# Encoder layer on one core: output projection by seven block products, residual held in DRAM and added to by accumulating transfers

## The chip, the core and the metric

The kernel runs on one core of a Trainium2 chip. The metric is the device time of one execution, in microseconds (us). The kernel before takes 936.28 us, the median of three runs (934.78 to 938.19).

## The reference

One encoder layer is applied to two sequences (`x_prompt`, `x_sample`) that share the weights. Each has 1024 positions and 1024 channels, in float32:

```
def _layer(x, p, ...):
    h = _rmsnorm(x, g_pre)
    z = einsum('bsd,de->bse', h, w_in)              # 1024 -> 3072
    a_val, a_gate, b_u, b_B, b_C, b_gate = split(z, 6, axis=-1)
    ya = _pool_mixer(a_val, w_pool, pool_scale) * silu(a_gate)
    yb = _short_conv(b_u, b_B, b_C, conv_w) * silu(b_gate)
    o = einsum('bse,ed->bsd', concatenate([ya, yb], axis=-1), w_out)   # 1024 -> 1024
    x = x + _rmsnorm(o, g_post)
    gate = sigmoid(einsum('bsd,de->bse', x, w_ple_gate))               # 1024 -> 1024
    e = einsum('bsk,kd->bsd', p, w_ple) * gate
    return x + _rmsnorm(e, g_ple)
```

## The kernel before

**Layout.** All tensors lie transposed: channels on the 128 partitions, positions along the free axis. A sequence `s` (0 the prompt, 1 the sample) has `KD`=8 channel tiles of 128 and `NCH`=2 chunks of `C`=512 positions. A float32 product is made of three: every operand is split into a high part (a cast on ACT, L145) and the rest (a subtraction on DVE, L146), and high by high, high by low and low by high are three matmuls of 128x128 by 128x512 (L284, L285, L286). An activation operand of two such parts is a "unit". An input for a unit that comes from DRAM goes through a tile `s` of 128x512, and there are `SBUFS`=6 of these. Everything else on positions lies in a pool of `TBUFS`=38 tiles `t` of 128x1024, which the units share. Weights come as tiles `wraw` of 128x1024 (three buffers) and are split in halves `whl` (eight buffers, `AHEAD`=5 halves split ahead).

**Stage A**, the input projection with both mixers: twelve pairs of channel tiles per sequence. The first pair of the prompt is done plainly. All others go through `pair_seven` (L455): seven block products of 12 matmuls, 84 per pair and both chunks, where plain products take 96. Its activation operands are sums and differences of blocks of h (`KINDS`: n11, n21, z, t1, t3, t4, n22, four units each, made once for a sequence); its weights (`pair_halves`, L195) are seven split halves and four sums on DVE. `emit` (L434) takes the results from PSUM, three of four with an add on DVE (L439, L441). The sample's operands are computed behind the prompt's stage A, stored in DRAM (`kept_...`) and loaded and split into units (`load_unit`) within the prompt's last pair: 28 units that take the place of the 28 of the prompt, each after the last product that reads the old one. The result y of stage A goes to DRAM (`yd`, 16 stores on POOL's queue).

**Stages B and C** then go sequence by sequence, with both chunks of B ahead of both of C. `stage_b` (L636) is the plain output projection: 8 channel tiles of 24 matmuls per chunk, on units of y that were loaded from `yd`; ACT scales the result by g_post out of PSUM (L654) and squares it. `norm_b` (L659) gets one over the root of the mean square (`rstd`, a product with ones, L301), loads x again from DRAM (16 tiles of 512 KB in all on SP's queue), multiplies and adds on DVE (L670, L671), and splits the new residual x1 into units. `stage_c` (L718) is the gate: 24 matmuls per piece (a channel tile of a chunk), a sigmoid on ACT (L738), the product with the p-projection, which the opening of the kernel had left in DRAM (`pled`, L739), and a square. `norm_c` (L772) scales (L786), adds x1 (L791) and stores y on SP's queue. The last `TAIL`=3 pieces of the last chunk are worked off in halves of 256 positions, in an order written out by hand.

**What sets the order.** The code is a program in order; `load` puts transfers on SP's queue and `bg_dma` on POOL's, both in program order (`pinned`). Work that no product waits for soon (`norm_b`, `norm_c`, loads of operands) is written as generators in a list `bg`; `tick` advances the first of them by a step after each product, and `drain` runs them to the end. `w_out` and `w_gate` are loaded once per chunk, 32 tiles each in all.

## Time and profile before

| | |
|---|---|
| median of 3 runs | 936.28 us (934.78 to 938.19) |
| profiled execution, its own time | 934.77 us |
| span of that execution | 932.6 us |
| TensorE (PE) busy | 894.6 us, 96% |
| VectorE (DVE) busy | 706.8 us, 76% |
| ScalarE (ACT) busy | 485.6 us, 52% |
| GpSimd (POOL) busy | 55.1 us, 6% |
| mean granted TensorE clock | 0.991 |

The profile is of one execution, 1.5 us under the median. Its span is the time from the first to the last recorded instruction. Stage A of the prompt ends near 310 us of it, stage A of the sample near 546, and the four chunk stages of each sequence fill the rest up to about 915, where the last piece's norm and stores begin. A group of instructions is named by its line, engine, operation and tiles (out<-in); idle time is put down to what ended it.

### The profile page before, as it was taken

To read this page: it belongs to the slowest core of one execution; us is meant where nothing else is said; L and a number is where in the kernel's file an instruction comes from. 1 tells how busy PE (TensorE), PEld (TensorE's weight loads), DVE (VectorE), ACT (ScalarE), POOL (GpSimd) and SP (SyncE) were. 2 spreads that over 40 slices of the span, in tenths; PEclk is the share of its full clock that TensorE was granted. 3 is DMA by queue.
4 is the path that set the end of the run, shared out by engine and by line. 5 is a ranking of instruction groups with operands and counts; after the bars stand their busy time and mean duration, and the time that the engine had idled before them with its cause. 6 is when DMAs were issued, how large, how long until landed. Compare 5 with 4: busy or idle time off the path is not lost.

```text
span 932.6 us, 11021 instructions
## 1 busy us (share of the span) xinstructions
PE 894.6 (96%) x3902; PEld 721.3 (77%) x3902; DVE 706.8 (76%) x1083; ACT 485.6 (52%) x829; POOL 55.1 (6%) x122
## 2 busy tenths in 40 slices
PE   6999999999999999999999989999999999999991
PEld 4787888888887788888888868878888787888881
DVE  5799999989588887665766764377878685969767
ACT  6967764333345643334333355465663745675643
POOL 0111112130000000000000000000000000000003
PEclk9999999999999999999999999999999999999996
DMA  9742545662316622122211174526146567262532
GB/s 329 293 181 76 195 147 173 217 238 84 112 48 202 226 91 69 68 82 76 68 68 69 68 257 150 181 87 229 69 181 225 203 185 289 91 225 69 188 129 90
DMA packets 48982, 140.49 MB, mean 151 GB/s; under 512 B 5664, under 2 KB 9248, under 8 KB 48928
## 3 DMA queue, kind: packets, MB, share of 16 engines
q1 hardware_dynamic: 39632, 107.23, 33.5%
q0 software_dynamic: 9152, 32.51, 9.5%
q8 instruction: 30, 0.49, 0.2%
q14 instruction: 24, 0.20, 0.1%
q10 hardware_dynamic: 144, 0.05, 0.0%
HBM read 107.27 MB, written 32.51 MB: 150 GB/s over the span
## 4 chain that ended last, share of the span: by engine, by line
PE 82%; DVE 8%; DMA 4%; ACT 3%; issue 2%; SPq 0%; DVEq 0%; ACTq 0%
PE z L286 27%; PE z L285 27%; PE z L284 27%; DVE t L791 1%; DVE t L786 1%; DVE u L146 1%; ACT u L145 1%; DMA s<-kept_t 1%; DMA s<-yd 1%; DMA s<-kept_n 1%; DVE t L833 1%; DMA t<-p_d 1%; DVE t L739 1%; DVE whl L146 1%; DMA t<-pled 0%
## 5 line engine op out<-in xcount | busy, mean ns | idle before, releaser
L284 PE MATMUL z<-u,whl 128*128 128x512 f32 (+1 forms) x1212 | 471.1, 390 | 4.8 <-ACT s L475 2.1
L285 PE MATMUL z<-u,whl 128*128 128x512 f32 (+1 forms) x1212 | 470.5, 389 | 1.4 <-DVE u L146 1.4
L286 PE MATMUL z<-u,whl 128*128 128x512 f32 (+1 forms) x1212 | 471.1, 389 | 0.5 <-DVE whl L146 0.5
L284 PEld LDWEIGHTS z<-u,whl 128*128 128x128 f32 x1212 | 227.2, 188 | 58.4 <-ACT s L475 3.4
L285 PEld LDWEIGHTS z<-u,whl 128*128 128x128 f32 x1212 | 227.6, 188 | 53.9 <-DVE u L146 2.8
L286 PEld LDWEIGHTS z<-u,whl 128*128 128x128 f32 x1212 | 227.7, 188 | 51.3 <-DVE whl L146 0.9
L146 DVE TENSOR_TENSOR whl<-wraw,whl 128x512 fp32r<-128x512 f32 x201 | 135.3, 687 | 46.3 <-ACT whl L145 45.7
L145 ACT CAST whl<-wraw 128x512 fp32r<-128x512 f32 x201 | 122.2, 620 | 73.7 <-PE z L286 63.7
L145 ACT CAST whl<-wsum 128x512 fp32r<-128x512 f32 x92 | 56.2, 620 | 70.8 <-PE z L286 35.7
L146 DVE TENSOR_TENSOR whl<-wsum,whl 128x512 fp32r<-128x512 f32 x92 | 62.8, 687 | 37.0 <-ACT whl L145 36.5
L145 ACT CAST u<-t 128x512 fp32r<-128x512 f32 (+1 forms) x105 | 61.6, 618 | 35.0 <-DVE t L671 12.8
L146 DVE TENSOR_TENSOR u<-t,u 128x512 fp32r<-128x512 f32 (+1 forms) x105 | 67.8, 680 | 15.3 <-ACT u L145 15.2
L330 DVE TENSOR_TENSOR t<-t 128x512 f32<-128x512 f32 (+1 forms) x59 | 39.1, 662 | 34.7 <-ACT t L329 34.1
L146 DVE TENSOR_TENSOR u<-s,u 128x512 fp32r<-128x512 f32 x60 | 39.3, 687 | 7.5 <-ACT u L145 7.2
L654 ACT ACTIVATE t<-z,par_sb 128x512 f32<-128x512 f32 x32 | 22.1, 689 | 44.0 <-PE z L286 44.0
L145 ACT CAST u<-s 128x512 fp32r<-128x512 f32 x60 | 35.8, 619 | 14.6 <-DMA s<-yd 7.4
L202 DVE TENSOR_TENSOR wsum<-wraw 128x512 f32<-128x512 f32 x46 | 31.6, 687 | 10.1 <-DMA wraw<-w_in_d 9.7
L284 PE MATMUL z<-u 128*128 128x512 f32 x64 | 26.0, 406 | 9.5 <-ACT u L145 9.5
L468 ACT COPY s<-z 128x512 f32<-128x512 f32 x23 | 13.5, 587 | 41.3 <-PE z L286 39.4
L475 ACT COPY s<-z 128x512 f32<-128x512 f32 x23 | 13.5, 586 | 41.2 <-PE z L286 41.2
L739 DVE TENSOR_TENSOR t<-t,s 128x512 f32<-128x512 f32 (+1 forms) x35 | 21.9, 641 | 15.8 <-ACT s L738 12.0
L738 ACT ACTIVATE s<-z 128x512 f32<-128x512 f32 (+1 forms) x35 | 19.6, 559 | 24.4 <-PE z L286 24.3
(85 smaller groups left out, 723.1 us busy)
## 6 DMA issues: line engine op xcount, KB each, us to landing
wraw<-w_in_d SPq DMA_DIRECT2D x48, 512.0 KB, 3.4
wraw<-w_out_d SPq DMA_DIRECT2D x32, 512.0 KB, 4.0
wraw<-w_gate_d SPq DMA_DIRECT2D x32, 512.0 KB, 3.4
pled<-t POOLq DMA_DIRECT2D x16, 512.0 KB, 3.8
t<-x_d POOLq DMA_DIRECT2D x16, 512.0 KB, 4.7
yd<-t POOLq DMA_DIRECT2D x16, 512.0 KB, 3.2
s<-yd SPq DMA_DIRECT2D x32, 256.0 KB, 4.9
t<-x_d SPq DMA_DIRECT2D x16, 512.0 KB, 7.7
```

Of the source, the lines that this page charges most:

```text
L145: nc.scalar.copy(out=hi, in_=src)
L146: nc.vector.tensor_tensor(out=lo, in0=src, in1=hi.bitcast(F32), op=ALU.subtract)
L202: nc.vector.tensor_tensor(out=t, in0=a, in1=b, op=ALU.add)
L284: nc.tensor.matmul(ps, wk[:, 0, kw, :], hi, start=a, stop=False, skip_group_check=on)
L285: nc.tensor.matmul(ps, wk[:, 0, kw, :], lo, start=False, stop=False, skip_group_check=on)
L286: nc.tensor.matmul(ps, wk[:, 1, kw, :], hi, start=False, stop=z, skip_group_check=on)
L330: nc.vector.tensor_tensor(out=acc, in0=acc, in1=tmp, op=ALU.add)
L468: nc.scalar.copy(out=u, in_=y)
L475: nc.scalar.copy(out=g, in_=y)
L654: nc.scalar.mul(og[d], z[i], col(G_POST + d))
L738: nc.scalar.activation(out=g, in_=z, func=AF.Sigmoid)
L739: nc.vector.tensor_tensor(out=e, in0=e, in1=g, op=ALU.mult)
```

## The change

The output projection (stage B) is computed by `pair_seven` too: four pairs of channel tiles per sequence, 84 matmuls each for both chunks. The stages now run as A of the prompt, A of the sample, B of the prompt, B of the sample, C of the prompt, C of the sample. What is new beside the product:

- `y_steps` loads the two halves of y of a group back on POOL's queue, makes four differences on DVE and stores them in DRAM (`ykept`); `load_y` loads and splits the 28 units of a sequence, within the last pair ahead of its stage B (A of the sample's last pair for the prompt, B of the prompt's last pair for the sample). The units n11, n21 and n22 are negated y.
- `Out` takes the results of stage B. The prompt's o is stored in DRAM (`od`) and loaded again; the sample's stays in SBUF.
- `residual` copies x to `x1d` in DRAM (POOL's queue). `norm_b` multiplies o by g_post and rstd (one DVE instruction of 128x1024 per channel tile, L718) and adds it to `x1d` by an accumulating transfer on POOL's queue (`bg_add`, 16 of 512 KB). The units of x1 are loaded from `x1d` and split: those of the prompt's first chunk within the last pair of B of the sample, the rest within stage C of the prompt.
- `norm_c` scales e and adds it to `x1d` by accumulating transfers too (24 of 256 KB), then copies `x1d` to y from DRAM to DRAM on POOL's queue (12 of 512 KB). Only the last chunk's tail loads x1 and adds on DVE as before.
- In stage C of the prompt a tile of `w_gate` serves both chunks, so 24 tiles of it are loaded instead of 32, and 16 of `w_out` instead of 32. A tile of `pled` is fetched one piece earlier than before.

```
+    def bg_add(out, in_):
+        pinned(nc.gpsimd.dma_start(out=out, in_=in_, accum_op=ALU.add))
...
+        for stage, n in (("A", NPAIR), ("B", KD // 2)):
+            for s in range(NSEQ):
+                for j in range(n):
+                    yield stage, s, j
...
+    raw_order.extend(w_gate[d] for i in range(NSEQ + 1) for d in range(KD))
...
+    def y_steps(s, j):
+
+        top, bottom = T()[:, :L], T()[:, :L]
+        bg_dma(top, yd[s][j])
+        bg_dma(bottom, yd[s][j + H])
...
+        for kind, out, p, q in (("t3", t, b, d), ("t1", b, b, a), ("z", d, d, b), ("t4", c, c, d)):
+            pinned(nc.vector.tensor_tensor(out=out, in0=p, in1=q, op=ALU.subtract))
+            bg_dma(ykept[s][kind][j], out)
...
+    class Out:
...
+        def put(self, d, c, ps, add, neg):
+            if d not in self.o:
+                self.o[d] = [T()[:, :L], NCH]
+            o = halves(self.o[d][0])[c]
+            emit(o, ps, add, neg)
+            a = halves(self.acc)[c]
+            add_square(a, o, small() if self.begun[c] else None, not self.begun[c])
...
+            if not self.left:
+                bg.append(norm_b(self.s, self.acc, self.kept))
...
+        for k, o in enumerate([kept[k] for k in range(KD)] if kept else ahead_of(load_o, KD, 2)):
+            yield
+            pinned(
+                nc.vector.scalar_tensor_tensor(
+                    out=o, in0=o, scalar=col(G_POST + k), in1=r, op0=ALU.mult, op1=ALU.mult
+                )
             )
...
+            bg_add(x1d[s][k // 2][:, :, k % 2, :], o.rearrange("p (c t) -> p c t", c=NCH))
...
+    def load_x1u(s, c, us, ks=range(KD)):
+        for k in ks:
+            us.append(load_unit(x1d[s][k // 2][:, c, k % 2, :]))
             yield
...
-        for d in range(KD - tail):
+        for i, (d, c) in enumerate(order):
+            while len(x1u[s][c]) < KD:
+                tick()
             pump(AHEAD)
-            piece(d, 0, C, next_w())
-            tick(2)
+            if d not in ws:
+                ws[d] = next_w()
+            piece(d, c, 0, C, ws[d])
...
+        def out(k):
+            bg_dma(y[s, c, :, k : k + 2, :], x1d[s][k // 2][:, c])
...
+                if x1 is None:
+                    bg_add(x1d[s][k // 2][:, c, k % 2, :], e)
...
+    def take_place(stage, s, n):
+
+        kind = KINDS[n]
+        if stage == "B" and s:
+            for i in range(2):
+                next(first_x1u, None)
+            return
+        for i in range(H):
+            if stage == "A" and s == 0:
+                h[1][kind][i] = load_unit(kept[kind][i])
+            else:
+                yk[1 - s if stage == "A" else 1][kind][i] = load_y(1 - s if stage == "A" else 1, kind, i)
...
+    bg.appendleft(load_x1u(0, 1, x1u[0][1]))
+    bg.extend(load_x1u(1, c, x1u[1][c]) for c in range(NCH))
+    first = [(0, 0), (1, 0), (0, 1), (1, 1)]
+    stage_c(0, first + [(d, c) for d in range(2, KD) for c in range(NCH)], 0)
+    stage_c(1, [(d, 0) for d in range(KD)] + [(d, 1) for d in range(KD - TAIL)], TAIL)
```

The first place is POOL's own order. Before, from the last stores of y at the end of stage A up to the tail's arithmetic (a number behind a name is only the tile's):

```order
L119 DMA yd_6_115<-t 128x1024
L491 MEMSET t 128x8
L492 MEMSET t 128x8
L119 DMA yd_3_112<-t 128x1024
L119 DMA yd_7_116<-t 128x1024
L779 ISA
L779 TENSOR_TENSOR t<-t 128x256
L780 TENSOR_TENSOR t<-t 128x256
```

After, the stretch of stage B of the sample, where o of the prompt is loaded (L121) and added to the residual (L124):

```order
L121 DMA t<-od_117 128x1024
L121 DMA t<-od_118 128x1024
L121 DMA t<-od_119 128x1024
L124 DMA x1d_0_125<-t 256x1x512
L121 DMA t<-od_120 128x1024
L124 DMA x1d_0_125<-t 256x1x512
L121 DMA t<-od_121 128x1024
L124 DMA x1d_1_126<-t 256x1x512
L121 DMA t<-od_122 128x1024
L124 DMA x1d_1_126<-t 256x1x512
```

POOL had nothing in stages B and C; now a chain of loads, accumulating transfers and, later, copies to y runs on its queue through both.

The second place is SP's queue where stage C of the prompt begins. Before:

```order
L114 DMA wraw<-w_out_d 128x1024 x8
L114 DMA t<-x_d 128x1024 x4
L114 DMA wraw<-w_out_d 128x1024 x2
L114 DMA wraw<-w_gate_d 128x1024 x6
L114 DMA t<-pled_0_0_85 128x1024
L114 DMA t<-x_d 128x1024 x4
```

After, with the loads of x1 (s<-x1d) among the weights:

```order
L116 DMA wraw<-w_out_d 128x1024 x4
L116 DMA wraw<-w_gate_d 128x1024 x3
L116 DMA s<-x1d_0_125 128x512 x2
L116 DMA s<-x1d_1_126 128x512 x2
L116 DMA wraw<-w_gate_d 128x1024
L116 DMA s<-x1d_2_127 128x512 x2
L116 DMA s<-x1d_3_128 128x512 x2
L116 DMA wraw<-w_gate_d 128x1024 x2
```

The loads of x are gone; in their place SP's queue holds loads that wait for accumulating transfers, with weights behind them.

The third place is SP's queue ahead of the tail. Before:

```order
L114 DMA wraw<-w_gate_d 128x1024 x2
L114 DMA y_d<-t 128x512 x2
L114 DMA t<-pled_1_1_98 128x1024
L114 DMA y_d<-t 128x512 x6
L114 DMA t<-pled_1_2_99 128x1024
L114 DMA t<-pled_1_3_100 128x1024
L114 DMA y_d<-t 128x256 x16
```

After:

```order
L116 DMA wraw<-w_gate_d 128x1024 x2
L116 DMA t<-pled_1_2_99 128x1024
L116 DMA t<-pled_1_3_100 128x1024
L116 DMA t<-x1d_0_129 128x1024
L116 DMA t<-x1d_1_130 128x1024
L116 DMA t<-x1d_2_131 128x1024
L116 DMA t<-x1d_3_132 128x1024
L116 DMA y_d<-t 128x256 x16
```

The stores of y have left this queue, and the two loads of pled stand ahead of everything that waits there.

## Rows read from the trace of the kernel before

**Rows 1.** The page: engines over the span, and PE's busy tenths in 40 slices.

```profile
PE 894.6 (96%) x3902; PEld 721.3 (77%) x3902; DVE 706.8 (76%) x1083; ACT 485.6 (52%) x829; POOL 55.1 (6%) x122
...
PE   6999999999999999999999989999999999999991
```

**Rows 2.** Windows by stage; columns are named in the first line.

```profile
core 0: us, PE busy (x) PEld busy (x) DVE busy (x) ACT busy (x) POOL busy (x), PEclk, DMA share, GB/s
100.00:150.00 50.00, 50.00 (x218) 40.49 (x217) 47.68 (x66) 33.39 (x50) 7.57 (x16) 1.00 0.46 154
...
296.00:330.00 34.00, 31.63 (x133) 24.49 (x133) 29.90 (x49) 23.25 (x41) 1.29 (x6) 1.00 0.69 231
536.00:556.00 20.00, 16.26 (x67) 11.95 (x66) 11.49 (x17) 9.47 (x16) 0.53 (x1) 1.00 0.78 248
560.00:893.00 333.00, 332.87 (x1433) 267.86 (x1432) 240.90 (x386) 195.76 (x330) 0.00 (x0) 1.00 0.49 170
893.00:915.00 22.00, 17.90 (x148) 17.26 (x146) 11.45 (x25) 10.51 (x22) 0.00 (x0) 1.00 0.21 72
```

**Rows 3.** PE's waits, 296 to 330: waiting line, releaser, us, times, longest.

```profile
PE z L284 <- ACT s L475: 1.4, 2, 1.0
PE z L284 <- ACT s L468: 0.6, 1, 0.6
PE z L284 <- DVE t L441: 0.4, 1, 0.4
```

**Rows 4.** ACT's waits, 285 to 330.

```profile
ACT u L145 <- DMA s<-kept_t: 4.0, 4, 1.3
```

**Rows 5.** PE's waits, 530 to 560.

```profile
PE z L284 <- ACT u L145: 1.6, 2, 1.3
PE z L285 <- DVE u L146: 1.4, 1, 1.4
```

**Rows 6.** The chain that ended last, at 549: start, us, what.

```profile
549.37 4.24 DMA s<-yd
```

**Rows 7.** Groups by line and shape: xcount | busy us, mean ns | idle before.

```profile
L146 DVE TENSOR_TENSOR whl<-wraw,whl 128x512 fp32r<-128x512 f32 x201 | 135.3, 687 | 46.3 <-ACT whl L145 45.7
...
L439 DVE SCALAR_TENSOR_TENSOR t<-z,s 128x512 f32<-128x512 f32 x30 | 20.6, 686 | 6.1 <-PE z L286 6.0
L671 DVE TENSOR_TENSOR t<-t 128x512 f32<-128x512 f32 x32 | 21.2, 685 | 0.0
L145 ACT CAST u<-s 128x512 fp32r<-128x512 f32 x60 | 35.8, 619 | 14.6 <-DMA s<-yd 7.4
```

**Rows 8.** DMA issues: queue, count, KB each, median us to landing.

```profile
t<-x_d POOLq DMA_DIRECT2D x16, 512.0 KB, 4.7
...
s<-yd SPq DMA_DIRECT2D x32, 256.0 KB, 4.9
t<-x_d SPq DMA_DIRECT2D x16, 512.0 KB, 7.7
...
s<-kept_n SPq DMA_DIRECT2D x12, 256.0 KB, 2.8
```

**Rows 9.** Timelines, DVE at 292 and POOL at 86: start, us, instruction.

```profile
292.05 2.49 DVE L146 TENSOR_TENSOR u<-s,u 128x512 fp32r<-128x512 f32 x4
...
86.18 1.45 POOL L119 DMA_DIRECT2D t<-x_d  x2 [3.26 <-DVE u L146]
```

**Rows 10.** Timeline of the tail: start, us, instruction, in brackets the idle time before.

```profile
885.41 9.10 SPq L114 DMA_DIRECT2D y_d<-t  x6
894.56 0.95 SPq L114 DMA_DIRECT2D t<-pled  x2
899.11 1.03 DVE L739 TENSOR_TENSOR t<-t,s 128x512 f32<-128x512 f32 x2 [2.55 <-DMA t<-pled]
905.08 0.39 PE L301 MATMUL psn<-u,ones 128*128 128x256 f32 x1 [0.84 <-ACT u L145]
```

More of the change, by code (lines that the diff above doesn't have):

```diff
@@ L298, in rstd_steps @@
         split(u[:, 0, :n], u[:, 1, :n], acc)
-        yield
+        for _ in range(wait):
+            yield
         ps = psn.tile([P, C], F32, name="psn")[:, :n]
@@ L343, in halves, with rstd_l, ahead_of @@
         return [t[:, c * C : (c + 1) * C] for c in range(NCH)]
-    def rstd_l(acc, tmp, out):
+    def rstd_l(acc, tmp, out, wait=1):
         for c in range(NCH):
-            yield from rstd_steps(halves(acc)[c], halves(tmp)[c], halves(out)[c])
-    def ahead_of(make, n):
-        cur = make(0)
+            yield from rstd_steps(halves(acc)[c], halves(tmp)[c], halves(out)[c], wait)
+    def ahead_of(make, n, depth=1):
+        got = deque(make(i) for i in range(depth))
         for i in range(n):
-            nxt = make(i + 1) if i + 1 < n else None
-            yield cur
-            cur = nxt
+            if i + depth < n:
+                got.append(make(i + depth))
+            yield got.popleft()
     def stats_steps(s, out):
@@ L659, in norm_b, with __init__, use, done @@
-    def norm_b(s, c, og, acc, tmp, x1, x1u):
-        for j in range(KD // 2):
-            t = T()
-            load(out=t[:, : 2 * C].rearrange("p (k t) -> p k t", k=2), in_=x[s, c, :, 2 * j : 2 * j + 2, :]
+                if self.s:
+                    bg.append(y_steps(self.s, self.g))
+    class Out:
+        def __init__(self, s):
+            self.s, self.acc, self.o = s, T()[:, :L], {}
+            self.left = 2 * KD
+            self.begun, self.kept = [False] * NCH, {}
+        def use(self, j):
+            return lambda m, c, ps, add=None, neg=False: self.put(2 * j + m, c, ps, add, neg)
+        def put(self, d, c, ps, add, neg):
[5 more added lines that the diff above has]
+            add_square(a, o, small() if self.begun[c] else None, not self.begun[c])
+            self.begun[c] = True
+            self.o[d][1] -= 1
+            if not self.o[d][1]:
+                self.done(d, self.o.pop(d)[0])
+            self.left -= 1
+            if not self.left:
+                bg.append(norm_b(self.s, self.acc, self.kept))
+        def done(self, d, o):
+            if self.s:
+                self.kept[d] = o
+            else:
+                bg_dma(od[d], o)
@@ new lines, in norm_b, with load_o @@
+    def norm_b(s, acc, kept):
+        r = T()[:, :L]
+        yield from rstd_l(acc, T()[:, :L], r, 3 if s else 1)
+        def load_o(k):
+            o = T()[:, :L]
+            bg_dma(o, od[k])
+            return o
+        for k, o in enumerate([kept[k] for k in range(KD)] if kept else ahead_of(load_o, KD, 2)):
+            yield
+            pinned(
+                nc.vector.scalar_tensor_tensor(
+                    out=o, in0=o, scalar=col(G_POST + k), in1=r, op0=ALU.mult, op1=ALU.mult
+                )
@@ L788, in norm_c @@
                 )
-            for k in ks:
-                e = es[k][:, cs]
-                nc.vector.tensor_tensor(out=e, in0=e, in1=x1[k][:, cs], op=ALU.add)
-                (load if n < C else store)(y[s, c, :, k, cs], e)
+                if x1 is None:
+                    bg_add(x1d[s][k // 2][:, c, k % 2, :], e)
+            if x1 is None:
+                if j:
+                    out(j - 2)
+            else:
+                for k in ks:
+                    e = es[k][:, cs]
+                    nc.vector.tensor_tensor(out=e, in0=e, in1=x1[k][:, cs], op=ALU.add)
+                    load(y[s, c, :, k, cs], e)
             yield
-    def blank():
-        return [[None] * KD for c in range(NCH)]
+        if x1 is None:
+            out(KD - 2)
     def run(steps):
@@ L920, in tile_hybrid_encoder, with residual @@
     load_pools()
+    def residual(s):
+        for j in range(KD // 2):
+            bg_dma(x1d[s][j], x[s, :, :, 2 * j : 2 * j + 2, :].rearrange("c p k t -> p c k t"))
+            yield
+            yield
+            yield
     r1 = T()[:, :L]
@@ L937, in after @@
                 product_done(LATER)
-            for i in range(H):
-                h[1][kind][i] = load_unit(kept[kind][i])
+            take_place(stage, s, n)
         else:
@@ L958, in tile_hybrid_encoder @@
             continue
-        steps = pair_seven(h[s], use)
+        steps = pair_seven((h if stage == "A" else yk)[s], use)
         next(steps)
@@ L963, in tile_hybrid_encoder @@
             if n:
[L964 removed]
+                after(*q, n + 1)
             else:
[L966 to L967 removed]
+                after(*q, 0), after(*q, 1)
+            if stage == "A" and i == 2 and n == 1:
                 grp.pool()
```

210 lines of the change are left out of this document (99 added, 111 removed).

## The prediction

> **What bounds the kernel now.** I read the page first: which engine is busy, and when. PE works 894.6 of 932.6 us, and its row of tenths shows no hole in the middle; the rest is the start and the last slice [rows 1]. So what counts is the number of matmuls and the places where PE stands. The windows by stage [rows 2] give both. In a full stretch, 100 to 150, 218 matmuls take 50.00 us, 0.2294 us each, at a granted clock of 1.00, which is the upper of the two levels (2.4 GHz). From 560 to 893, all of stages B and C but the ends, PE is idle for 0.13 us of 333: nothing there waits, and nothing of DVE, ACT or DMA in it costs time as it lies. PE stands at three places after the start: 2.4 us at the hand-over from the prompt's stage A to the sample's (296 to 330), 3.7 us from stage A to stage B (536 to 556), 4.1 us in the tail (893 to 915).
>
> The waits name the causes. At the hand-over PE waits for ACT copies out of PSUM [rows 3], and these stand behind casts of units that wait for their loads (4.0 us at one kind [rows 4]). Between A and B, PE waits for the units of y [rows 5], and the chain there goes through a load of y of 4.24 us [rows 6]. In the tail two loads of pled stand on SP's queue behind six stores of y that hold it for 9.10 us; DVE waits 2.55 us for them, and the norm's product 0.84 [rows 10].
>
> I take the profiled execution as the base: 934.77 us, 1.5 below the median of 936.28.
>
> **Matmuls.** Stage B goes from 2 sequences x 2 chunks x 8 tiles x 24 = 768 to 2 x 4 pairs x 84 = 672, so 96 fewer. At 0.2294 us [rows 2] this is −22.0 us. It holds in full if the stretches stay as dense as 560 to 893 is now.
>
> **Other engines in stage B.** In a pair DVE has 7 splits, 4 sums of weights, 3 emits and 4 squares, 18 instructions x 0.69 us [rows 7] = 12.4 us, against 84 x 0.2294 = 19.3 us of PE. In stage A, 47.7 of 50 us of DVE hid under a full PE [rows 2]. The differences of y (32 instructions x 0.69 = 22 us) lie in stage A of the sample and in B of the prompt, where that slack covers them; the 32 multiplications and the 32 additions of norm_b now (0.685 each, L671's row standing for both [rows 7]) become 16 of twice the length. Cost 0. Without that cover it would be the 22 us, spread over two stages; I see no such place.
>
> **The gap from A to B.** The prompt's stage B no longer begins with y that has just been stored: it comes two stages later. The 3.7 us [rows 2] go, and the sample's y is loaded 4 pairs later as well. −3.7. What comes late next is the hand-over.
>
> **Two new hand-overs.** In the last pair ahead of each stage B, 28 units are loaded, cast and subtracted while their predecessors are read, as at the hand-over that exists now, where 28 units cost 2.4 us. The load on DVE is about the same: two pairs at 19 and 28 units, 66 instructions, at 0.62 us back to back (four in 2.49 [rows 9]) = 41 us, against 38.5 us of PE for two pairs. So there is a little more work than cover. Two things are heavier. The units n11, n21 and n22 come from `yd`, whose loads took 4.9 us where kept_n's took 2.8 [rows 8]. And in stage B the six `s` tiles also hold the squares and the copies of PSUM. Lower bound 0 (the units' casts get to DVE and ACT earlier than the products need them), upper bound worked out as a rival below. I take 3.0 us for each, nearest to the 2.4 us measured for the same 28 units: +6.0.
>
> **The waits on accumulating transfers.** SP's queue meets loads of x1 from B of the sample's last pair on; each waits until both adds of its tile have landed, and behind them stand the weights of stage C. The trace shows no accumulating transfer. Bounds for one of 512 KB, from issue to landing: 4.7 us if it is no dearer than a load of x of the same shape on POOL's queue, 9.6 us if it reads first and writes then, a load of 4.9 and another of 4.7 [rows 8]. I take 6, nearer to the lower end, as reading and writing can overlap; the highest row of 512 KB on any queue is 7.7 [rows 8].
>
> The first point where it can hurt: between the last multiplication of the prompt's norm_b and the split of its unit stand 25 instructions on DVE, x 0.60 us at the fastest = 15.0 us. Off go the issue on POOL (0.72, half of the pair's 1.45 [rows 9]), the unit's load (4.9 [rows 8]) and its cast (0.62 [rows 7]): 8.8 us are left for the add. Beyond that each us is paid at stage C's start. At 6 us it costs 0, at the upper bound of 9.6, 0.8. The adds before the last have more room; the sample's eight lie under stage C of the prompt, 16 pieces x 24 x 0.2294 = 88 us. POOL's issues are 0.72 us each, and nothing else needs that queue until the tail. The Trainium skill, page "Collectives: The Full Stack", section "The bandwidth ceiling: the fold count and why AG ≠ RS ≠ AR", says that an add in the DMA engines needs two reads of source and so runs at about half a copy's rate. By it an add would be an estimated 2 x 4.7 = 9.4 us, 0.6 over the margin, and the sum 0.6 higher; no run here shows it yet.
>
> **Stage C of the prompt** begins with two pieces of chunk 0, and then needs all eight units of chunk 1 for the third. Three of the eight can go through free `s` tiles ahead; the other five are loaded and split once the pieces have begun. PE needs a new unit every three matmuls, 0.69 us, and ACT and DVE can make one every 0.62 [rows 9], so only the first of the five can be late: it is needed 3 x 0.69 = 2.1 us into the third piece, and before it four instructions of the second piece's eviction (about 0.65 each, two of them on ACT) and its own cast and split (0.62 + 0.69 [rows 7]) are done, 3.9 us. That is 1.8 us late if all of it runs one after the other, and not late if two overlap. Bounds 0 and 2, I take the middle: +1.0. Shared tiles of w_gate lower the load on SP, DVE and ACT here, which I price at 0, as none of them bounds this stage [rows 2].
>
> **Loads that leave SP.** The 16 loads of x (7.7 us each, beside weights [rows 8]) and most stores of y leave its queue. No PE idle depended on them between 560 and 893, so 0.
>
> **The tail.** The pled tiles are fetched a piece earlier, ahead of what blocked them; the waits of 2.55 on DVE and 0.84 on PE [rows 10] go. On PE only the second lay on the way to the norm: −0.9, rounded with the issue. The end, 20 us of DVE and POOL arithmetic, keeps its form. What is new: POOL's adds and copies of chunk 0 stand ahead of its arithmetic in the tail, and the x1 that it adds must have come from DRAM. For chunk 0's adds two transfers of 256 KB and their issues, 2 x (0.55 x 6) + 1.8 = 8.4 us, lie under 4 pieces, about 22 us of PE. Cost 0.
>
> **Sum.** −22.0 −3.7 +6.0 +0.0 +1.0 −0.9 = −19.6 us. On the profiled execution 915.2; on the median 936.28 − 19.6 = 916.7, the forecast.
>
> **Rivals.**
>
> *The hand-overs stall on the `s` tiles.* 28 loads go through six tiles, of which squares and copies take one and a half to two and a half, so 3.5 to 4.5 are free. Each load holds its tile for its landing, its cast and its subtraction, 4.9 + 0.62 + 0.69 = 6.2 us [rows 7, 8]. 28 x 6.2 / 3.5 = 50 us, where about 38 of PE lie beside it: 12 us late, against 28 x 6.2 / 4.5 = 39 us, in time. For it: PE already waits behind such loads [rows 3, 4], and ACT waited 14.6 us over the 60 unit casts [rows 7]. Against it: with the same six tiles the hand-over costs only 2.4 us now. With +9 in B (against 3) and +5 in A (against 3), the time is 916.7 + 8 = 924.7.
>
> *The hand-overs are free.* y is in DRAM long before, so the loads wait for nothing but a free tile, and the pairs of stage B have no mixers beside them on DVE. Against it: the kept tiles of h lie ready now too, and PE still loses 2.4 us [rows 2]. Then −6.0: 910.7.
>
> *Slower: the accumulating transfers are slow.* One mechanism at one place: the adds of the prompt delay the units of x1 at the start of C, and those of chunk 0 of the sample delay the tail, through POOL's queue. With an add of L us for 512 KB, the first costs L − 8.8, the second 2 x 0.55 L + 1.8 − 23 where that is positive. It eats the gain of 19.6 from L of about 25 on (16.2 + 6.3 = 22.5). At L = 30 it is 21.2 + 11.8 = 33 us: 949. For it: no transfer here that reads and writes DRAM and adds has been seen, and the queue was idle before. Against it: the slowest transfer of this size, in the fullest stretch, took 7.7 us [rows 8], a third of the threshold.
>
> *No gain.* The 96 matmuls go, but waits of the same size take their place; that is the same two places with 20 us of stalls between them, and the time is 936. No row adds up to it.
>
> **How the numbers follow.** Forecast .62; hand-overs stall .18; hand-overs free .12; slow transfers .05; no gain .03. A measurement of this kernel can tell about 0.3%, 2.8 us, from no change. Faster by more: .62 + .18 + .12 = .92; within: .03; slower by more: .05. The range runs from 908 (910.7, less 1.0 for stage C at its lower bound and 2.55 − 0.84 = 1.7 if the whole of DVE's wait in the tail was on the path) to 928 (stalling hand-overs, and the ends of the unknown costs: 0.8 of the add, 1 of stage C, 1.5 of hand-over), leaving out the .05, the .03 and the edges of the others.
>
> **What would show it.** PE's matmuls 96 fewer, and the windows of stage B at 19.3 us a pair. PE idle at three hand-overs: near 2.4, 3 and 3 us, and its waits there naming ACT copies and unit casts. Landing of the adds against 8.8 us; no wait of SP for them that reaches PE at the start of C; at the third piece of C about 1 us. In the tail no wait of L739 for pled, and POOL's arithmetic not late. Wrong would be: a PE idle of more than 10 us anywhere after the start, a matmul of stage B dearer than 0.23 us, or an add over 10 us.

## The result, and the profile of the changed kernel

The changed kernel takes 971.46 us, the median of four runs (970.26 to 973.77), against 937.1 for four runs of the kernel before beside it: a ratio of 1.0373, interval 1.0344 to 1.0403. It is slower by 34 us, where the forecast was 20 us faster. The profiled execution has a span of 972.0 us, 39.4 more than the 932.6 of before.

The page of the changed kernel, as in [rows 1]; below them its granted clock in tenths:

```profile
PE 884.8 (91%) x3806; PEld 710.3 (73%) x3806; DVE 724.6 (75%) x1099; ACT 489.5 (50%) x833; POOL 139.9 (14%) x246
...
PE   6999999999999999999999989989599999089990
...
PEclk9999999999999999999999989999889999589995
```

The 96 matmuls are gone (3902 records before, 3806 now), but PE's share fell from 96 to 91%, and its row of tenths, which had no hole in the middle, now has a 5 and, further on, a 0 and an 8 side by side. Where PE stands, the granted clock falls with it: to 8 and to 5 tenths in the same slices.

The windows of the stretches that [rows 2] showed and of the new holes. Columns are as there: us, busy us and (in brackets) instructions of PE, PEld, DVE, ACT, POOL, then the granted clock, DMA share and GB/s:

```profile
296.00:330.00 34.00, 32.49 (x139) 25.38 (x138) 29.93 (x48) 22.41 (x40) 2.83 (x7) 1.00 0.81 269
...
530.00:560.00 30.00, 28.48 (x122) 22.41 (x121) 27.52 (x44) 21.42 (x38) 0.54 (x1) 1.00 0.74 232
560.00:600.00 40.00, 36.04 (x143) 28.40 (x142) 28.26 (x45) 18.81 (x34) 5.93 (x11) 0.91 0.53 191
...
680.00:720.00 40.00, 29.46 (x101) 22.44 (x100) 24.80 (x35) 12.07 (x22) 8.77 (x10) 0.83 0.84 186
...
760.00:800.00 40.00, 40.00 (x174) 32.39 (x173) 27.52 (x36) 20.59 (x31) 3.23 (x3) 1.00 0.55 137
800.00:840.00 40.00, 24.41 (x106) 19.43 (x104) 6.18 (x10) 6.22 (x11) 5.42 (x5) 0.84 0.66 127
840.00:880.00 40.00, 25.24 (x102) 20.12 (x103) 29.64 (x47) 29.62 (x47) 6.34 (x8) 0.77 0.69 188
```

A full stretch of 40 us holds 174 matmuls, 0.230 us each, as before. Two places fall far below it. One is 680 to 720, stage B of the sample, with 101 matmuls: 73 fewer, or 17 us. The other is 800 to 880, where stage C passes from the prompt to the sample, with 208 of 348: 140 fewer, or 32 us. PE's idle time is only part of that. In the second place PE is busy for 49.65 us with 208 matmuls, 0.24 us each, and up to 0.43 right behind the hole, where the granted clock is 0.50 (856 to 858), the lower level. A smaller hole, 560 to 600, lies ahead of all the adds and is taken up further down.

What PE waited for, 300 to 972 (waiting line, releaser, us, times, longest):

```profile
PE psn L308 <- ACT u L150: 34.2, 2, 30.4
PE z L290 <- ACT s L502: 6.7, 2, 3.8
PE z L290 <- DVE t L475: 5.9, 4, 4.0
PE z L292 <- DVE whl L151: 5.3, 2, 4.0
```

One wait of 30.4 us, for the cast of a norm's input on ACT, is most of the loss. Three views follow it back: ACT (790 to 860) stands at casts of units of x1 that wait for their loads, SP (690 to 860) at these loads, which wait for accumulating transfers, and POOL (690 to 860) between these transfers, for nothing that the profile shows:

```profile
ACT u L150 <- DMA s<-x1d: 42.3, 9, 6.9
...
SPq L116 <- DMA x1d<-t: 63.6, 10, 8.2
...
POOL x1d L124 <- issue: 51.6, 8, 9.8
```

POOL's timeline shows what that is (start, us, instruction, in brackets the idle time before it and what ended it). First the prompt's adds (`x1d<-t`, 512 KB) with loads of o between them, then some of the sample's, then the 256-KB adds of `norm_c`:

```profile
673.17 1.12 POOL L124 DMA_DIRECT2D x1d<-t  x1 [7.56 <-DVE t L718]
673.78 1.09 POOL L121 DMA_DIRECT2D t<-od  x1
679.88 1.11 POOL L124 DMA_DIRECT2D x1d<-t  x1 [5.01 <-issue]
...
686.71 1.10 POOL L124 DMA_DIRECT2D x1d<-t  x1 [5.14 <-issue]
...
774.17 1.08 POOL L124 DMA_DIRECT2D x1d<-t  x1 [48.05 <-DVE t L718]
...
827.99 1.10 POOL L124 DMA_DIRECT2D x1d<-t  x1 [5.66 <-issue]
865.46 2.62 POOL L124 DMA_DIRECT2D x1d<-t  x3 [36.37 <-DVE t L867]
```

Most adds of 512 KB come 6.7 to 7.3 us apart, of which POOL is busy for 1.1; three of the fourteen gaps are longer, up to 10.9 us. The sample's eight go from 774.2 to 828.0, 54 us. Three adds of 256 KB go out within 2.62 us. The DMA issues, answering [rows 8] (KB each, median us to landing):

```profile
x1d<-t POOLq DMA_DIRECT2D x16, 512.0 KB, 6.5
s<-x1d SPq DMA_DIRECT2D x32, 256.0 KB, 4.4
...
x1d<-t POOLq DMA_DIRECT2D x24, 256.0 KB, 8.7
```

The chain of waits shows the end of it (start, us, what): the last add, a load of x1 behind it, and the norm's product that PE had waited for since 824.4.

```profile
827.99 6.45 DMA x1d<-t
...
836.34 6.89 DMA s<-x1d
...
854.76 0.79 PE psn L308
```

An add lands 6.5 us after its issue (the median; 6.4 to 10.5). The prediction took 6. So the latency was right, and what was wrong is that the next one is not issued until then: in the sample's chain each goes out 0.3 us after the one before it has landed. In stage B of the sample it costs by another way: the loads of o stand on POOL's queue behind the adds, and DVE, in its fixed order, waits for them (672 to 730):

```profile
DVE t L718 <- DMA t<-od: 15.7, 5, 3.9
```

### The profile page after: what moved, and what is told of

Same layout as the page of the kernel before. It is cut to its first block, busy times and chain, and to the rows that moved or that the text cites. A ratio compares the mean times of both kernels' runs of the same rounds, so it can differ in the third digit from the quotient of the medians.

```text
span 972.0 us, 11143 instructions
## 1 busy us (share of the span) xinstructions
PE 884.8 (91%) x3806; PEld 710.3 (73%) x3806; DVE 724.6 (75%) x1099; ACT 489.5 (50%) x833; POOL 139.9 (14%) x246
## 4 chain that ended last, share of the span: by engine, by line
PE 62%; issue 18%; DVE 7%; DMA 6%; ACT 4%; POOL 2%; SPq 0%; DVEq 0%; POOLq 0%; ACTq 0%
PE z L290 21%; PE z L291 21%; PE z L292 21%; POOL x1d L124 2%; DVE u L151 1%; DMA s<-kept_t 1%; ACT u L150 1%; DMA t<-yd 1%; DVE t L927 1%; DMA s<-x1d 1%; DMA s<-ykept_t 1%; DMA x1d<-t 1%; DMA t<-p_d 1%; DVE t L647 1%; DVE t L867 0%
## 5 line engine op out<-in xcount | busy, mean ns | idle before, releaser
L290 PE MATMUL z<-u,whl 128*128 128x512 f32 (+1 forms) x1180 | 463.7, 394 | 18.1 <-ACT s L502 6.7
L292 PE MATMUL z<-u,whl 128*128 128x512 f32 (+1 forms) x1180 | 461.6, 392 | 5.8 <-DVE whl L151 5.8
L291 PE MATMUL z<-u,whl 128*128 128x512 f32 (+1 forms) x1180 | 461.7, 392 | 0.2 <-DVE u L151 0.2
L150 ACT CAST whl<-wsum 128x512 fp32r<-128x512 f32 x124 | 75.5, 619 | 98.0 <-PE z L292 45.8
L150 ACT CAST whl<-wraw 128x512 fp32r<-128x512 f32 x145 | 88.4, 619 | 54.3 <-PE z L292 46.0
L151 DVE TENSOR_TENSOR whl<-wraw,whl 128x512 fp32r<-128x512 f32 x145 | 97.9, 686 | 15.4 <-ACT whl L150 15.3
L151 DVE TENSOR_TENSOR u<-s,u 128x512 fp32r<-128x512 f32 x92 | 61.3, 688 | 59.6 <-ACT u L150 59.2
L151 DVE TENSOR_TENSOR whl<-wsum,whl 128x512 fp32r<-128x512 f32 x124 | 84.3, 687 | 27.4 <-ACT whl L150 26.7
L150 ACT CAST u<-s 128x512 fp32r<-128x512 f32 x92 | 55.2, 618 | 66.9 <-DMA s<-x1d 51.5
L124 POOL DMA_DIRECT2D x1d<-t x40 | 38.3, 1026 | 209.6 <-issue 67.4
L151 DVE TENSOR_TENSOR u<-t,u 128x512 fp32r<-128x512 f32 (+1 forms) x73 | 46.8, 679 | 10.7 <-ACT u L150 10.4
L336 ACT ACTIVATE s<-t 128x512 f32<-128x512 f32 (+1 forms) x59 | 35.7, 609 | 30.3 <-DVE t L800 15.0
L121 POOL DMA_DIRECT2D yd<-t x16 | 8.7, 543 | 236.7 <-DVE t L610 137.6
```

Source lines behind the costliest of these rows:

```text
L124: pinned(nc.gpsimd.dma_start(out=out, in_=in_, accum_op=ALU.add))
L150: nc.scalar.copy(out=hi, in_=src)
L151: nc.vector.tensor_tensor(out=lo, in0=src, in1=hi.bitcast(F32), op=ALU.subtract)
L290: nc.tensor.matmul(ps, wk[:, 0, kw, :], hi, start=a, stop=False, skip_group_check=on)
L291: nc.tensor.matmul(ps, wk[:, 0, kw, :], lo, start=False, stop=False, skip_group_check=on)
L292: nc.tensor.matmul(ps, wk[:, 1, kw, :], hi, start=False, stop=z, skip_group_check=on)
```

## The experiments

The theory after these readings, Q: POOL's queue holds an accumulating transfer until the one before it has landed, and the chain of eight, mostly 6.8 us apart, is what PE waits for. The rival, M: memory and DMA engines are slow there for all transfers. Times are medians beside the kernel before on the same chip, which took 935.3 to 936.3 us in all five groups of runs. A time that stands without a ratio is one execution; repeated executions of one kernel lay 4 to 12 us apart here, so a few us between single ones prove nothing. Diffs are against the changed kernel unless another is named.

### Plain stores in place of the adds

```
-            bg_add(x1d[s][k // 2][:, :, k % 2, :], o.rearrange("p (c t) -> p c t", c=NCH))
+            bg_dma(x1d[s][k // 2][:, :, k % 2, :], o.rearrange("p (c t) -> p c t", c=NCH))
```

> The changed kernel with the 16 accumulating transfers of norm_b (512 KB each) made plain stores of the same shape to the same place; the residual is left out of x1, everything else is done. Theory Q: an accumulating transfer holds POOL's queue until the one before it has landed, so 16 of them go one after the other, 6.8 us apart, and that chain makes PE wait 30.4 us for the norm ahead of stage C of the sample and about 10 us in the last pairs of stage B of the sample. Then the stores are issued within about 1.5 us of each other, both stalls go, and the time falls from 971 to 920 to 930 us. Rival M: the memory and the 16 DMA engines are what is slow there (share 0.6 to 0.84 in these windows); then stores of the same bytes stay more than 4 us apart, and the time stays over 955.

It took 921.24 us. POOL's timeline, at the sample's stores:

```profile
759.83 0.68 POOL L121 DMA_DIRECT2D x1d<-t  x1 [3.79 <-DVE t L718]
761.03 0.68 POOL L121 DMA_DIRECT2D x1d<-t  x1 [0.52 <-DVE t L718]
762.45 0.67 POOL L121 DMA_DIRECT2D x1d<-t  x1 [0.75 <-ACT whl L150]
...
774.03 0.68 POOL L121 DMA_DIRECT2D x1d<-t  x1 [5.13 <-DMA t<-pled]
```

The first stores follow DVE at 1.2 to 1.4 us, and the stretch from 720 to 880 is full of matmuls. The last one was held too, until the fifth had landed at 773.7: three plain stores were on their way then (the load of pled that the line names is none of its inputs). So stores of these bytes are not slow there, as M had it; a store moves less than an add, though, and the run with rows of 4 KB below settles M with the adding left in. Without the adds' pace the kernel is where the forecast had put it, within 4.5 us.

### The sample's adds alone

```
-            bg_add(x1d[s][k // 2][:, :, k % 2, :], o.rearrange("p (c t) -> p c t", c=NCH))
+            (bg_dma if s else bg_add)(x1d[s][k // 2][:, :, k % 2, :], o.rearrange("p (c t) -> p c t", c=NCH))
```

> The same edit for the sample's eight transfers of norm_b alone (its residual is left out of x1); the prompt's eight still accumulate. By Q only the stall of 30.4 us ahead of the sample's stage C goes, with the low clock behind it: 935 to 942 us, and the stalls between 680 and 710 stay as they are. By M it stays over 960.

934.53 us, 0.5 under the range that Q gave. The prompt's adds still come some 6.8 us apart there. So of the 50.2 us between 971.5 and 921.2, these runs give 36.9 to the sample's eight adds and 13.3 to the prompt's eight. When the starts of the same matmuls are compared in the three traces, it is 32 and 13: some 5 us of the 36.9 were lost by 600, ahead of any add. Nearly all of that is the hole of 560 to 600, behind a load of y that landed 7.5 us after its issue and here 4.9.

### Adding in SBUF

```
+            xk = T()[:, :L]
+            bg_dma(xk.rearrange("p (c t) -> p c t", c=NCH), x[s, :, :, k, :].rearrange("c p t -> p c t"))
...
+            pinned(nc.vector.tensor_tensor(out=o, in0=o, in1=xk, op=ALU.add))
-            bg_add(x1d[s][k // 2][:, :, k % 2, :], o.rearrange("p (c t) -> p c t", c=NCH))
+            bg_dma(x1d[s][k // 2][:, :, k % 2, :], o.rearrange("p (c t) -> p c t", c=NCH))
```

> norm_b adds in SBUF again: x is loaded on POOL's queue beside o, DVE adds (16 instructions of 128x1024, 1.28 us each, 20 us in all), and x1 goes to DRAM by a plain store; the copy of x to DRAM ahead of it goes. Seven block products, the order of the stages and norm_c stay as changed. By Q both stalls go and DVE's 20 us are hidden: 918 to 932 us, faster than before (937) by 1 to 2%. By M the loads of x in the same place keep the stalls: over 950.

942.65 us, ratio 1.0105 (1.0047 to 1.0163). The adds' pace was gone, and yet the time stayed 21 us over that with plain stores; the expected range was missed. The windows of that run (columns as above) show that the loss in stage B of the sample stayed, while that at 800 to 840 is small:

```profile
680.00:720.00 40.00, 28.97 (x109) 22.18 (x110) 30.51 (x42) 14.97 (x27) 8.63 (x13) 0.83 0.80 266
...
800.00:840.00 40.00, 36.56 (x153) 29.25 (x152) 30.96 (x50) 27.74 (x46) 3.56 (x4) 0.96 0.74 221
```

DVE's additions wait in order for x (5.3 us at two of them) and PE once 8.5 us for a result that ACT takes out of PSUM late. The two loads and one store per tile on POOL's queue put a wait where the add had been. In the traces 15 us of the loss lie in stage B of the sample and 5 at the norm ahead of its stage C; why they are so large is settled no further than that.

### Adds of half the size

```
-            bg_add(x1d[s][k // 2][:, :, k % 2, :], o.rearrange("p (c t) -> p c t", c=NCH))
+            for c in range(NCH):
+                bg_add(x1d[s][k // 2][:, c, k % 2, :], halves(o)[c])
```

> Each accumulating transfer of norm_b in two of 256 KB, one per chunk, so 32 of them; nothing is left out. If the queue holds one accumulating transfer at a time whatever its size, each takes about 3.4 us or a little more, and the time is 968 to 985. If it holds them by their bytes or rows, three are in flight together as in norm_c, the eight of the sample take about 45 us and not 55, and the time is 955 to 966.

941.43 us, under both ranges: one at a time it is not. POOL's timeline, some of the prompt's adds, then the first and the last of the sample's sixteen:

```profile
687.80 0.89 POOL L124 DMA_DIRECT2D x1d<-t  x1 [0.68 <-issue]
689.08 0.87 POOL L124 DMA_DIRECT2D x1d<-t  x1 [0.38 <-issue]
...
760.53 1.74 POOL L124 DMA_DIRECT2D x1d<-t  x2 [58.56 <-DVE t L718]
765.05 1.76 POOL L124 DMA_DIRECT2D x1d<-t  x2 [2.78 <-DVE t L718]
771.74 0.87 POOL L124 DMA_DIRECT2D x1d<-t  x1 [4.93 <-issue]
...
797.92 0.87 POOL L124 DMA_DIRECT2D x1d<-t  x1 [0.74 <-issue]
```

Up to three are in flight together. The sample's sixteen take 37 us and not 54 for the same bytes, and PE's longest wait at the norm falls from 30.4 to 13.1 us. So Q was too simple: something in a transfer's size or form decides whether the next may follow.

### Rows, bytes or the adding itself

A 512-KB add of this kernel is 256 rows of 2 KB (two chunks of 128 channels; a row is one unbroken piece of DRAM), a 256-KB add 128 rows of 2 KB. Two runs tell rows from bytes. The first lays `x1d` out so that both chunks of a channel are one row of 4 KB; an add is still one transfer of 512 KB:

```
-        [tc.dram_tile([P, NCH, 2, C], F32, name=f"x1d{s}_{j}") for j in range(KD // 2)] for s in range(NSEQ)
+        [tc.dram_tile([P, 2, L], F32, name=f"x1d{s}_{j}") for j in range(KD // 2)] for s in range(NSEQ)
...
-            bg_add(x1d[s][k // 2][:, :, k % 2, :], o.rearrange("p (c t) -> p c t", c=NCH))
+            bg_add(x1d[s][k // 2][:, k % 2], o)
```

with the other accesses to `x1d` written to match, and x copied to it by 16 transfers in place of 8.

> The changed kernel with the residual laid out in DRAM so that both chunks of a channel tile are one row: an add of norm_b is still one transfer of 512 KB, in 128 rows of 4 KB and not 256 rows of 2 KB. Nothing is left out. If the number of rows in flight is what POOL's queue can't take, adds of 128 rows go like the 256-KB ones (also 128 rows): the next is issued before the last has landed, some 4 us apart and not 6.8, and the time is 935 to 950. If the bytes or the accumulating itself hold the queue, they stay 6.5 us or more apart: 965 to 975.

932.4 us, ratio 0.9961 (0.9939 to 0.9982): under the range that was expected, and faster than before by 0.4%. POOL's timeline at the same place:

```profile
762.21 0.84 POOL L124 DMA_DIRECT2D x1d<-t  x1 [3.66 <-DVE t L718]
763.41 0.83 POOL L124 DMA_DIRECT2D x1d<-t  x1 [0.35 <-DVE t L718]
764.82 0.86 POOL L124 DMA_DIRECT2D x1d<-t  x1 [0.58 <-ACT whl L150]
...
773.21 0.85 POOL L124 DMA_DIRECT2D x1d<-t  x1 [1.68 <-issue]
```

These are 512 KB each. The first of them go out 1.2 and 1.4 us apart, as fast as DVE gives them; from then on three are on their way, and each of the last four goes out 0.3 us after the oldest has landed. The eight take 23 us from the first issue to the last and not 54. They now land 9.3 us after their issue. As many bytes are added at the same place as in the changed kernel, so M is out: the memory's rate did not set the pace. The second run cuts each add in two of 256 KB, but by columns, so that each has 256 rows of 1 KB:

```
-            bg_add(x1d[s][k // 2][:, :, k % 2, :], o.rearrange("p (c t) -> p c t", c=NCH))
+            n = C // 2
+            for q in range(2):
+                bg_add(
+                    x1d[s][k // 2][:, :, k % 2, q * n : (q + 1) * n],
+                    o.rearrange("p (c t) -> p c t", c=NCH)[:, :, q * n : (q + 1) * n],
+                )
```

> The changed kernel with each add of norm_b cut in two of 256 KB by columns, 256 rows of 1 KB each, where the earlier cut in two was by chunks, 128 rows of 2 KB. Nothing is left out. If the rows in flight are what POOL's queue can't take, each of these 32 adds waits for the one before it to land, the sample's sixteen take more than the 54 us of the eight whole ones, and the time is 975 to 1030. If the bytes are, they go like the other 256-KB adds: 938 to 948.

1009.46 us. POOL's timeline:

```profile
834.59 1.09 POOL L124 DMA_DIRECT2D x1d<-t  x1 [3.46 <-issue]
839.44 1.10 POOL L124 DMA_DIRECT2D x1d<-t  x1 [3.76 <-issue]
843.94 1.09 POOL L124 DMA_DIRECT2D x1d<-t  x1 [3.40 <-issue]
```

Half the bytes, 256 rows, and again one at a time, 4.5 to 4.9 us apart. So it is the rows that decide, and not the bytes or the adding as such. Three adds of 128 rows go out together, two of 256 rows never did. (Every transfer of 256 rows here is two pieces of 128, so rows and pieces are not told apart.)

### The sample's chain started sooner

With whole adds, the sample's rstd and multiplications were moved ahead within stage C of the prompt, and the loads of its units back (`nb` is the sample's `norm_b`; its rstd also waits one step and not three):

```
+            if s == 0 and i < 2:
+                for _ in range(3):
+                    next(nb, None)
+            tick(0 if s == 0 and 5 <= i < 9 else 3)
-            tick(3)
```

> The changed kernel with whole adds of 512 KB and only the sample's norm_b moved ahead as in the two runs before. By Q the sample's chain keeps its 8 x 6.8 = 54 us but starts near 748 and not at 774, so it ends near 803 instead of 828, while PE gets to the sample's stage C near 816: the wait of 30.4 us falls to 0 to 6, and the time to 935 to 945. The adds of the prompt keep their stalls near 680 to 710. If whole adds hold up SP's queue wherever they are, more than 950.

960.34 us; the range was missed. The chain began at 762.1, where 774.2 was before and 748 expected, so 12 us sooner, and the time fell by 11. That is the chain's own rule at work (whatever it starts sooner is gained), but the move did not reach as far as was planned: the multiplications wait for rstd, whose norm product stands among the pieces on PE.

The same move with 256-KB adds (the run before, in its expectation, is the one with adds of half the size), and with o loaded four tiles ahead in place of two:

> Adds of 256 KB as in the run before, and the sample's norm_b moved ahead: its rstd is made beside the first two pieces of stage C of the prompt, its multiplications and adds beside the next three, its units are loaded from the tenth piece on. With 256-KB adds the sample's chain took 37 us (760 to 798) and PE waited 13.1 us for it, with the low clock behind that. Theory Q: the chain now starts about 15 us sooner, so this wait goes: 922 to 930 us, faster than before. Rival: the wait is not the chain's but that of the queue of SP or ACT at this place, which the move only shifts: 938 to 946.

> As the run before, with o of the prompt loaded four tiles ahead of the multiplications in place of two. With two ahead DVE waits 8.0 us for these loads, which stand behind adds on POOL's queue, and PE loses about 5 us there (679 to 696). If the loads' place on the queue is the cause, most of this goes: 3 to 6 us less than the run before, 918 to 926. If the tiles for it are not free in time, no difference.

936.79 us (ratio 1.0001, 0.9982 to 1.0021) and 941.75 us (1.006, 1.004 to 1.0081), both missed. In both PE has no wait left between 760 and 880; the wait of 13.1 us is gone. But the earlier rstd now stands where stage C of the prompt begins, and the window there is no longer full in the first of the two:

```profile
720.00:760.00 40.00, 35.67 (x146) 27.98 (x147) 26.13 (x40) 27.48 (x43) 2.63 (x3) 0.96 0.54 169
...
760.00:800.00 40.00, 40.00 (x174) 32.36 (x173) 25.33 (x36) 16.90 (x30) 11.27 (x13) 1.00 1.05 251
```

28 matmuls fewer than full, 6.4 us, so half of the gain was given back. Loading o four tiles ahead did nothing for DVE's waits for it (7.4 us) and cost 5 us. The tiles for it were not free: two of the loads, at 675.1 and 684.5, went out 0.65 us after an add had landed, though nothing else was left on POOL's queue.

### Where the loads of o stand

With 256-KB adds, o loaded on SP's queue (`load` for `bg_dma` in `load_o`), and the same with the sample's residual added in SBUF:

> 256-KB adds as in the run that took 941.4, with o of the prompt loaded on SP's queue and not behind the adds on POOL's. DVE waited 8.0 us there for these loads, and PE about 5. If their place behind the adds is the cause, DVE's waits for od fall under 2 us and the time by 4 to 7 us: 934 to 938. If not: 940 to 943, or more where they hold up the weights on SP's queue.

> As the run just before for the prompt; for the sample, whose o lies in SBUF, x is loaded and added there by DVE and x1 goes to DRAM by a plain store, so that no accumulating transfer is left ahead of the sample's stage C. The wait of 13.1 us there goes, and with it the low clock behind it: 918 to 926, faster than before. If x's loads come as late as the adds did, a part of it stays: 927 to 934.

945.24 us (1.008, 1.005 to 1.011) and 937.62 us (1.001, 0.9994 to 1.0026). Both were missed. DVE's waits for o fell to 1.7 and 0.5 us, as expected, but another wait took their place at once. Loaded sooner, o holds tiles of the common pool, and a result of stage B finds none until an add has landed (DVE's waits in the first of the two, 655 to 725):

```profile
DVE t L475 <- DMA x1d<-t: 8.8, 2, 8.4
DVE u L151 <- ACT u L150: 2.6, 4, 0.9
DVE t L718 <- DMA t<-od: 1.7, 1, 1.7
```

### The hand-overs and the s tiles

The kernel with plain stores, with `SBUFS` 5 for 6:

> The kernel with plain stores in norm_b (the residual left out of x1; it took 921.2 us) with five tiles s in place of six. If the loads of the 28 units at the hand-overs are limited by these tiles, as the rival of the prediction has it, one tile of 3.5 to 4.5 free ones less makes each of the three hand-overs 6 to 12 us dearer: 935 to 955. If not, 921 to 925.

936.96 us, 15.7 more, so the loads at the hand-overs do hang on these tiles. By the starts of the same matmuls in the two traces, one tile fewer costs 6.5 us at each of the first two hand-overs and about 1 at the third; 2 us are lost at the start of the kernel. With six, the price is near what the forecast took.

### What was left

The kernel with rows of 4 KB, with the sample's rstd a step sooner (`wait` 1 for 3) and its units loaded later (`tick(0 if s == 0 and 7 <= i < 10 else 3)`):

> The kernel with rows of 4 KB (932.4 us), with the sample's rstd one step sooner and its units loaded from the eleventh piece of the prompt's stage C on, so that casts of units that wait for adds don't stand ahead of the sigmoids on ACT (two waits of 6.1 and 7.7 us there, and PE waited 4.2 us at the norm behind them). If these waits are the cause, PE's 4.2 us go, and with the low clock behind it the time falls to 924 to 929. If the units then come too late for the sample's stage C, 932 to 940.

935.58 us (0.9999, 0.9982 to 1.0016), the worse of the two outcomes that were expected. Of the 4.2 us ahead of the sample's stage C 0.6 are left, and the window 800 to 880 is full. But the end came no sooner: from its first matmul on, the tail took 48.0 us, where it was 40.8 with rows of 4 KB alone. In the tail POOL's queue still works off adds and copies of the chunk before, and only then its arithmetic; DVE is done by then (POOL's last copy and first multiplication, then the last instruction of DVE, of a span of 932.1):

```profile
916.26 0.72 POOL L121 DMA_DIRECT2D y_d<-x1d  x1 [2.34 <-DMA x1d<-t]
917.08 0.75 POOL L856 TENSOR_TENSOR t<-t 128x256 f32<-128x256 f32 x1
...
915.79 0.42 DVE L878 TENSOR_TENSOR t<-t 128x256 f32<-128x256 f32 x1
```

So the next run took that arithmetic off POOL, and one more loaded o three tiles ahead:

```
-TAIL_POOL = (4, 5, 6, 7), (7,)
+TAIL_POOL = (), ()
```

> The kernel before (935.6 us; rows of 4 KB, the sample's units loaded later) with all of the tail's arithmetic on DVE and none on POOL. There POOL's queue issued its last copy to y at 916.3 and only then began its ten instructions, while their input lay ready from about 906, and DVE was done at 916.2 of 932.1. If POOL's queue sets the end, DVE now does ten more instructions of about 0.4 us, ends near 920, and the time falls by 6 to 9 us: 926 to 930, faster than before. If the stores of y or the copies land last anyway, 933 to 937.

> As the run before, with o of the prompt loaded three tiles ahead and not two. DVE waits about 7 us for these loads in stage B of the sample, and PE loses 4 us there. If a tile is free for it: 2 to 4 us less than the run before; if not, as with four ahead: 2 to 5 us more.

927.51 us (ratio 0.9919, 0.9897 to 0.9942) and 926.73 us (0.9917, 0.989 to 0.9945). POOL's queue had set the end: the tail is back to 41.5 us in the first of the two. Both are faster than before by 0.8%; the third tile makes no difference that these runs tell. With rows of 4 KB, the units later and the tail on DVE, the change's idea holds: it gains 8 of the 20 us. The kernel before was not run with its own tail on DVE, so how much of the 8 that edit alone would give there is not shown.

## Why the prediction was wrong

**Matmuls**: right. 96 fewer at the same 0.23 us; in each full window of 40 us there are 174.

**Other engines**: nearly right. The differences of y cost one wait that was priced at 0: DVE waited 5.1 us for the last y (at 573) and PE 4.0 behind it, which is the 560 to 600 window's hole; that load of y landed 7.5 us after its issue. In the other runs this wait of PE was at most 2.1 us, and why it was longer here is not shown. The profiled execution is the slowest of the four.

**The gap from A to B**: right. The 3.7 us of [rows 2] are gone; 530 to 560 is idle for 1.5.

**The hand-overs**: right in size. PE waited 1.5 us at the one into stage B of the prompt and 3.9 at the one into the sample's (1.0 and 2.9), where 3.0 each had been taken. The tiles that the rival named do set it, as the run with five shows, but six were just enough.

**The accumulating transfers**: this is the step that failed. Its latency, 6 us, was right (6.5). The failed sentence is "POOL's issues are 0.72 us each, and nothing else needs that queue until the tail". That price came from plain loads of x [rows 8, 9]. They have 256 rows too, but are no adds, and the kernel before never had more than three of them on their way. An add of 256 rows isn't issued while another is in flight, so the eight were issued over 54 us, and POOL stood between them. The margin of 8.8 us was worked out for the last add of the prompt alone, with those ahead of it taken as landed. And the sample's eight were left with "more room", 88 us, without asking when in these 88 us they start: they began at 774, PE came to the norm behind them at 824, and the chain with what follows it took until 855. "Nothing else needs that queue" failed as well: the loads of o stood on it between the adds. By the runs, 36.9 us are the sample's chain (32 by the traces), 13.3 the prompt's; 50.2 of the 55 between forecast and result.

**Stage C of the prompt**: right. 1.1 us at its third piece (0.85 and 0.23, waits for units).

**The tail**: half right. The first norm product of 256 positions came 11.4 us after the tail's first matmul, where it was 12.2, so the 0.8 us were gained, and 0.5 of it was still there at the second. But POOL's arithmetic, which had begun with its input, at 0.6 us behind ACT's first multiplication (914.64 and 915.23 in the trace of before), now began 4.7 us behind it (951.53 and 956.25), after its adds and copies; "Cost 0" for POOL's queue was wrong. In all, the tail took 41.8 us from its first matmul to the end of the span and not 39.7.

**The rivals**: the one that ended slower, "the accumulating transfers are slow", named the right instruction, the right places and POOL's queue, at .05. Its rule was wrong: it priced the latency of one, with a threshold of 25 us, where the pace of eight decides, and the threshold is lower. From the chain's start to PE's arrival are 824 − 774 = 50 us; from the last landing (834.4) to the norm's product (854.8) 20 more go to loads, casts and sigmoids; so eight adds have 30 us, 3.8 each. They took 60 (774.2 to 834.4), 7.5 each. The argument against it ("the slowest transfer of this size, in the fullest stretch, took 7.7 us [rows 8], a third of the threshold") compared a latency with the wrong number; and 7.7 is the median of that row, whose slowest took 10.5.

## What to carry to other kernels

A transfer that goes into a chain has two prices, how long until it lands and how soon the next may follow. The second has to be read from rows of the same kind (engine, operation, rows per transfer), and where there is none, take the landing for it, so that a chain costs the count times the landing. The layout can change it: the same bytes in half the rows went three at a time here. Write the chain's start and its consumer's arrival next to it. And whatever is put on a queue behind such a chain (here the loads of o and the tail's arithmetic) waits with it.

## What the runs showed of the hardware

Accumulating transfers from POOL's queue to DRAM, by rows and bytes of one:

| rows x bytes | run | most on their way | apart | landing |
|---|---|---|---|---|
| 256 x 2 KB | as changed | one | 7.7 us | 6.5 us |
| 256 x 1 KB | by columns | one | 5.1 us | 4.3 us |
| 128 x 2 KB | by chunks | three | 2.5 us | 6.3 us |
| 128 x 4 KB | long rows | three | 3.3 us | 9.3 us |
| 256 x 2 KB, plain store | no adding | three | 2.7 us | 5.5 us |

The count and the mean distance are those of the sample's chain, the landing is the median over norm_b. POOL is busy for 1.1 us at an add of 256 rows and for 0.86 at one of 128. The adding has its price: the fastest add of 256 rows landed in 6.4 us, the fastest plain store of the same form in 3.2. The medians are nearer (6.5 and 5.5 us), but the stores went up to three at a time and the adds alone.

What holds an issue back can be worked out from the issues and landings in the traces. Add up the rows of all transfers of POOL's queue that are on their way, an add's rows twice. In none of the 17 traces, with 3392 transfers, does an issue bring this sum above 896. Where POOL had stood idle for more than 0.3 us and went on 0.25 to 0.42 us after a landing, the sum would have come to 1024 or more without that landing in 531 of 597 cases. An add of 256 rows counts 512 and so finds no room beside another; an add of 128 rows and a plain transfer of 256 count 256, and three of them go together. So it was with the 1-MB copies of x (256 rows of 4 KB, plain): three were issued at once, and the two after them waited 4.3 and 3.6 us for nothing that the profile shows. The timeline has them as

```profile
377.19 1.36 POOL L121 DMA_DIRECT2D x1d<-x_d  x2
...
383.60 0.64 POOL L121 DMA_DIRECT2D x1d<-x_d  x1 [4.29 <-issue]
```

in the changed kernel.

The Trainium skill, page "Collectives: The Full Stack", section "The bandwidth ceiling: the fold count and why AG ≠ RS ≠ AR", says of the adds of a ReduceScatter that each piece takes two read descriptors, where a copy takes one, and that they so run at about half a copy's rate. The fastest landings agree with it (6.4 and 3.2 us), and so does the sum in which an add's rows count twice. The prediction's estimate by that rule, 9.4 us, had doubled a load of 4.7 us, and the median add took 6.5. What in the chip the sum stands for no run here shows.
